# A hybrid decoder trunk whose split weights are made by casting and accumulating transfers

## The chip, the core and the metric

The kernel runs on one core of a Trainium2 chip. The time is device microseconds from launch to end, the median of several runs of the same program; a profile is one further execution under the hardware profiler. Engines are named as in the profile: PE (TensorE), DVE (VectorE), ACT (ScalarE), POOL (GpSimd) and SP (SyncE, which here only issues transfers).

## What is computed

Two layers, each a mixer of four head groups beside each other (retention, differential attention, Mamba-2 SSD, mLSTM) with one input projection and one output projection in common, on 512 tokens of width 1024, all in float32:

```python
for l in range(DEPTH):                      # 2
    u = rmsnorm(h, norm_w[l])
    proj = einsum('bsd,de->bse', u, w_in[l])          # 1024 -> 7696 columns
    ret_p, diff_p, ssd_p, ml_p = split_cols(proj, ...)
    mix = concatenate([ret_out, diff_out, ssd_out, ml_out], axis=-1)   # 2048 columns
    h = h + einsum('bse,ed->bsd', mix, w_out[l])
return rmsnorm(h, final_norm_w)
```

## The kernel before

**Split operands.** The projections' matmuls take operands of the type `float32r`. Each operand is cut in two: a high part, which is the value cast to float32r, and a low part, which is the value less the high part. A product is three matmuls that add up in PSUM: high x high, low x high and high x low. For the activations the parts are `uh` and `ul` (transposed, 8 pieces of 128 features by 512 tokens), or `mh` and `ml` for a mixer's output; for the weights they are `whi` and `wlo`.

**Blocks.** The input projection is cut into 15 blocks of 512 columns; a block is 8 pieces (k = 0 to 7) of 128 x 512. `load_block` (L326) asks `split_w` (L321) for two pieces at a time: one transfer of 512 KB on SP's queue into a tile `raw` (two buffers), then for each piece a cast on ACT into `whi` (L316) and a subtraction into `wlo` (L318), on POOL for even k and on DVE for odd k. `whi` and `wlo` have ten buffers of 128 x 512 each, so ten pieces, 1.25 blocks, can be in the chip. All of it stands at high priority in the scheduler.

**Use.** `proj_tok` (L396) makes a block's output for four tiles of 128 tokens, `proj_feat` (L413) for four tiles of 128 columns. A tile is 24 matmuls of 512 columns into one PSUM bank (`pspj`, two banks), in the order of the pieces: high part with uh, high part with ul, low part with uh, then the next piece. So a piece's buffers are in use from the first tile of a block to its last. An evacuation follows each tile: DVE or ACT reads `pspj`, for instance L478 (a convolution over time), L498 (rotary embedding) or L436 (silu). `out_proj` (L520) works in the same way: for each half of the 1024 output columns 4 pieces, 12 matmuls a tile, and L547 adds the tile to `h`.

**Order.** The program writes out TensorE's order itself: `filler` runs the steps of a layer in the order of the list `ORDER` (mv, gates, mq, mk, mlstm, mo, mz, dk, dq, diff, dv, dz, m, xs, bc, ssd, d, rqk, sz, rv, rz, ret, s, r; the one-letter steps are the output projections), and at each `yield` of a projection the parts of the mixers that have come due are put between its matmuls. The other engines' order is made by a scheduler from priorities; each engine, and each transfer queue, then works through its instructions strictly in that order. In layer 0 the first block (mv, in `start`, L330) is written out by hand on all engines, with its own tiles and a list that says in which order high and low parts are used in the first tile.

Of the kernel before, what the change touches and what calls it, by code (L numbers as in the profile page):

```python
# [11 lines left out]
F32 = mybir.dt.float32  # L12
F32R = mybir.dt.float32r
# [5 lines left out]
P = 128  # L19
# [9 lines left out]
# column offsets of the combined input projection  # L29
# [5 lines left out]
# the 512 column blocks in the order in which they are used  # L35
# [7 lines left out]
# columns of the row parameters that every partition gets  # L43
# [3 lines left out]
# the order of the steps of a layer  # L47
# [3 lines left out]
# the pieces of a block of weights whose low parts GpSimd computes  # L51
POOL_K = (0, 2, 4, 6)

# tiles that hold the queries' parts
QS = 4

# how much work of TensorE is issued before work that depends on other engines
# [5 lines left out]
# columns of the constants  # L63
# [31 lines left out]
class Trunk:  # L95
    def __init__(self, ctx, tc, aps, dbg=None):
        self.tc, self.nc = tc, tc.nc
        self.x, self.win, self.wg, self.wout, self.nrm, self.rows, self.convp, self.cst, self.out = aps
        self.dbg = dbg or {}
        mk = lambda n, b, **k: ctx.enter_context(tc.tile_pool(name=n, bufs=b, **k))  # L100
        self.cp = mk("cp", 1)
        self.pool = mk("pool", 1)
        self.ps = mk("ps", 2, space=bass.MemoryType.PSUM)
        self.n = 0
        # the order of TensorE's work: tasks come due on a clock of emitted TensorE time
        self.clk = 0.0
        self.heap = []
        self.done = set()
# [16 lines left out]
    def spawn(self, gen, delay=0.0):  # L125
        """Runs a generator; what it yields is the delay until it goes on."""
        def step():
            for w in gen:
                self.later(w, step)
                return  # L130
        self.later(delay, step)
# [44 lines left out]
    def setup(self):  # L176
# [13 lines left out]
        # keeps TensorE busy until the first data come in, so that it runs at its full clock  # L190
# [42 lines left out]
    def load_nw(self, l, eng):  # L233
        """The weights of a norm of h, on every partition."""
        self.nw = [self.t("bcm", [P, 512], bufs=2) for _ in range(2)]
        for half in range(2):
            eng.dma_start(out=self.nw[half],
                          in_=self.nrm[l:l + 1, half * 512:(half + 1) * 512].to_broadcast([P, 512]))
# [72 lines left out]
    def split_half(self, raw, j, vector=False):  # L311
        nc = self.nc
        hi = self.t("whi", [P, 512], F32R, bufs=10)
        lo = self.t("wlo", [P, 512], F32R, bufs=10)
# [6 lines left out]
    def split_w(self, src, g):  # L321
        raw = self.t("raw", [P, 2, 512], bufs=2)
        self.nc.sync.dma_start(out=raw, in_=src)
        return [self.split_half(raw[:, j, :], 2 * g + j not in POOL_K) for j in range(2)]

    def load_block(self, name):  # L326
        b = BIDX[name]
        return [q for g in range(4) for q in self.split_w(self.win[self.l, b, :, 2 * g:2 * g + 2, :], g)]

    def start(self, evac):  # L330
        """The first block: the norm of x, and the weights, as they come in."""
# [9 lines left out]
        with self.tc.manual_schedule(engines={E.Activation, E.DVE, E.Pool, E.SP}):  # L341
# [3 lines left out]
            for k in range(KD):  # L345
                if k < 4:
                    if k % 2 == 0:
                        r = self.t("raw", [P, 2, 512], bufs=2)
                        nc.sync.dma_start(out=r, in_=self.win[0, b, :, k:k + 2, :])
                    raw.append(r[:, k % 2, :])  # L350
                else:
                    raw.append(self.t("z", [P, 512], bufs=8))
                    nc.sync.dma_start(out=raw[k], in_=self.win[0, b, :, k, :])
                if k == 3:
                    load(1)
# [4 lines left out]
            # on VectorE or GpSimd  # L360
            split = lambda k, v, h=False: w.append(self.split_half(raw[k], v, h))
            n = [self.norm_in_t(t) for t in range(NT)]
            # the products with the weights' high parts (0) and low parts (1), as these come in
# [32 lines left out]
    def proj_tok(self, name, evac, w=None, toks=range(NT), order=None):  # L396
        nc = self.nc
        w = w or self.load_block(name)
        for t in toks:
# [4 lines left out]
            for k, parts in order or [(k, (0, 1)) for k in range(KD)]:  # L404
                for part in parts:
# [7 lines left out]
    def proj_feat(self, name, evac):  # L413
        nc = self.nc
        w = self.load_block(name)
        for f in range(4):
            p = self.psum("pj")
            fs = slice(f * P, (f + 1) * P)
            for k in range(KD):
                hi, lo = w[k][0][:, fs], w[k][1][:, fs]  # L420
                self.mm(p, lhsT=hi, rhs=self.uh[:, k, :], start=(k == 0), stop=False)
                self.mm(p, lhsT=hi, rhs=self.ul[:, k, :], start=False, stop=False)
                self.mm(p, lhsT=lo, rhs=self.uh[:, k, :], start=False, stop=(k == KD - 1))
                yield
            evac(f, p)

    # evacuations
    def ev_silu(self, dst, tag, bufs, nwt=None):
        """2 * silu(z), times a row weight."""
# [57 lines left out]
    def ev_rope(self, sink, scale=1.0):  # L487
        """Rotates the heads' halves; the features lie on the partitions."""
# [21 lines left out]
    def finish_mix(self, mix):  # L510
        """Transposes of a mixer's output, in high and low parts, for the output projection."""
# [8 lines left out]
    def out_proj(self, g, mixt, tok_outer=False, after=None, cut=False, heads=False):  # L520
        nc = self.nc
        gi = GROUPS[g]
        w = [[x for q in range(2) for x in self.split_w(self.wout[self.l, gi, half, :, 2 * q:2 * q + 2, :], 2 * half + q)]
# [4 lines left out]
        for t, hf in order:  # L528
# [5 lines left out]
            for c0, c1 in zip(cuts, cuts[1:]):  # L534
# [4 lines left out]
                for k in range(4):  # L539
                    hi, lo = w[hf][k]  # L540
                    mh, ml = m(t, k)
                    self.mm(p, lhsT=mh, rhs=hi[:, cs], start=(k == 0), stop=False)
                    self.mm(p, lhsT=ml, rhs=hi[:, cs], start=False, stop=False)
                    self.mm(p, lhsT=mh, rhs=lo[:, cs], start=False, stop=(k == 3))
                    yield
# [15 lines left out]
    def gates(self):  # L561
# [20 lines left out]
        # log1p(exp(-|x|)) = 2 atanh(z / (2 + z)), z = exp(-|x|)  # L582
# [31 lines left out]
        # SSD factors  # L614
# [12 lines left out]
        # rows  # L627
# [19 lines left out]
        # running maxima: rows 0.. G, 32.. mu, 64.. G at the end of the chunk  # L647
# [44 lines left out]
    def bcast(self, src, n, t, tag, bufs):  # L692
        """Rows of src, columns of chunk t, on every partition."""
# [9 lines left out]
    def mlstm(self, v, th, zs, q, k, res):  # L703
# [5 lines left out]
        for t in range(NT):  # L709
# [47 lines left out]
            # denominators  # L757
# [18 lines left out]
            # r / 2 * rsqrt(r^2 / 4 * var + eps)  # L776
# [112 lines left out]
    def retention(self, qk, v, zs, res):  # L889
# [6 lines left out]
        for t in range(NT):  # L896
# [6 lines left out]
            # heads on different rows of the array write different banks  # L903
# [55 lines left out]
    def split_k(self, dst):  # L959
        """High and low parts of a head's keys, one above the other, for each of its two maps."""  # L960
# [13 lines left out]
    def split_q(self, x):  # L974
        """The high parts of a head's queries, on both halves of the partitions, and the low parts."""
# [108 lines left out]
    def layer(self, l, last):  # L1084
        """The steps of a layer that keep TensorE busy, and the mixers that run between them."""
# [40 lines left out]
        def end():  # L1126
# [7 lines left out]
            # mLSTM  # L1134
# [8 lines left out]
            # differential attention  # L1143
# [6 lines left out]
            # SSD  # L1150
# [5 lines left out]
            # retention  # L1156
# [7 lines left out]
    # columns of the last tokens' halves  # L1164
# [34 lines left out]
def _layout(i):  # L1199
    """The inputs, cut and reordered into the pieces that the kernel loads."""  # L1200
# [36 lines left out]
```

## Time and profile before

| | |
|---|---|
| median of 3 runs | 1088.46 us (1086.24 to 1088.56) |
| span of the profiled execution, from its first to its last instruction (the only time known of it) | 1091.0 us |
| mean granted TensorE clock | 0.984 |
| busy: PE, DVE, ACT, POOL | 1043.6, 714.8, 492.0, 392.9 us |
| bytes moved by transfers | 95.53 MB, 88 GB/s over the span |

A group's line in the profile reads: line of the kernel, engine, operation, output<-inputs by the program's names, shapes, count | busy us, mean ns of one | idle us of the engine just before them, and what ended most of it. A line of the timeline reads: start in us, duration, engine, line, operation, count, and in brackets the idle time of that engine before it with its releaser. In the order of instructions, names carry buffer numbers, and an xN at the end stands for N equal instructions in a row.

### The profile page before, as it was taken

The numbers are of one execution on the slowest core, as the hardware profiler recorded it, in microseconds if no ns is written. First come the engines' busy times: TensorE is split into PE (matmuls) and PEld (weight loads), VectorE is DVE, ScalarE is ACT, GpSimd is POOL, SyncE is SP. The second block draws the span as 40 slices with busy tenths as digits, with TensorE's granted clock in tenths as the row PEclk, the third lists the DMA queues.
The fourth block names the chain that finished last, engine by engine and source line by source line (L and its number), as shares of the span: only waits on it lengthen the run. The fifth ranks groups of instructions, "written<-read, shape, count | busy, mean of one in ns | idle before, by whom it ended". The sixth has DMA issues, their size and how long they took to land.

```text
span 1091.0 us, 14197 instructions
## 1 busy us (share of the span) xinstructions
PE 1043.6 (96%) x5052; PEld 848.7 (78%) x5052; DVE 714.8 (66%) x1369; ACT 492.0 (45%) x1082; POOL 392.9 (36%) x369
## 2 busy tenths in 40 slices
PE   7999989999999899999999999999999999999997
PEld 6778878777788787787887788787877877787776
DVE  5686676567787767445556867664687886773454
ACT  4444337655554344332344442484555542543332
POOL 3322445324323354225132234533252343542341
PEclk8999999999999999999999999899999999999999
DMA  7332313321312323332122322222231223223202
GB/s 283 102 100 85 97 49 97 96 77 57 92 46 79 106 68 97 108 119 72 39 82 74 116 89 86 78 77 77 79 101 55 78 87 107 71 85 115 78 20 77
DMA packets 39143, 95.53 MB, mean 88 GB/s; under 512 B 3592, under 2 KB 16520, under 8 KB 38944
## 3 DMA queue, kind: packets, MB, share of 16 engines
q1 hardware_dynamic: 38064, 93.18, 26.8%
q10 hardware_dynamic: 1008, 1.44, 0.4%
q8 instruction: 39, 0.64, 0.2%
q14 instruction: 32, 0.26, 0.1%
HBM read 92.47 MB, written 2.15 MB: 87 GB/s over the span
## 4 chain that ended last, share of the span: by engine, by line
PE 79%; DVE 11%; DMA 3%; issue 3%; ACT 3%; POOL 1%; SPq 0%; ACTq 0%; POOLq 0%; DVEq 0%
PE pspj L115 64%; PE psacc L115 6%; PE psS L115 5%; PE psS L119 4%; DVE wlo L318 3%; DMA raw<-in_w_in_dram 2%; DVE w L826 2%; DVE e L478 1%; ACT whi L316 1%; DMA cst<-in_consts_dram 1%; DVE w L721 0%; ACT e L496 0%; POOL s L207 0%; DVE z L436 0%; DVE ft L498 0%
## 5 line engine op out<-in xcount | busy, mean ns | idle before, releaser
L318 POOL TENSOR_TENSOR wlo<-raw,whi 128x512 fp32r<-128x512 f32 x150 | 206.5, 1380 | 358.8 <-ACT whi L316 231.7
L318 DVE TENSOR_TENSOR wlo<-raw,whi 128x512 fp32r<-128x512 f32 x150 | 173.7, 1159 | 89.4 <-ACT whi L316 76.9
L115 PE MATMUL pspj<-whi,uh 128*128 128x512 f32 x512 | 209.5, 409 | 8.5 <-DVE ft L498 8.2
L316 ACT CAST whi<-raw 128x512 fp32r<-128x512 f32 x300 | 175.8, 619 | 91.9 <-DMA raw<-in_w_in_dram 54.7
L115 PE MATMUL pspj<-whi,ul 128*128 128x512 f32 x512 | 201.8, 394 | 0.0
L115 PE MATMUL pspj<-wlo,uh 128*128 128x512 f32 x512 | 201.5, 395 | 0.2
L115 PE MATMUL pspj<-uh,whi 128*128 128x512 f32 x448 | 182.0, 406 | 9.3 <-DVE e L478 4.9
L115 PE MATMUL pspj<-uh,wlo 128*128 128x512 f32 x448 | 177.3, 396 | 1.2 <-POOL wlo L318 1.2
L115 PE MATMUL pspj<-ul,whi 128*128 128x512 f32 x448 | 176.4, 394 | 0.0
L115 PEld LDWEIGHTS pspj<-whi,uh 128*128 128x128 f32 x512 | 97.6, 191 | 31.0 <-DVE ft L498 9.7
L115 PE MATMUL pspj<-whi,mh 128*128 128x512 f32 (+1 forms) x260 | 107.4, 413 | 10.7 <-DVE h L547 8.0
L115 PEld LDWEIGHTS pspj<-wlo,uh 128*128 128x128 f32 x512 | 96.9, 190 | 22.7 <-DVE wlo L318 1.0
L115 PEld LDWEIGHTS pspj<-whi,ul 128*128 128x128 f32 x512 | 97.8, 191 | 18.2 <-DVE ul L306 0.2
L115 PEld LDWEIGHTS pspj<-uh,whi 128*128 128x128 f32 x448 | 85.6, 191 | 28.9 <-issue 6.1
L115 PE MATMUL pspj<-whi,ml 128*128 128x512 f32 (+1 forms) x260 | 102.2, 393 | 0.0
L115 PE MATMUL pspj<-wlo,mh 128*128 128x512 f32 (+1 forms) x260 | 102.2, 393 | 0.0
L115 PEld LDWEIGHTS pspj<-uh,wlo 128*128 128x128 f32 x448 | 85.4, 191 | 21.1 <-POOL wlo L318 2.5
L115 PEld LDWEIGHTS pspj<-ul,whi 128*128 128x128 f32 x448 | 85.6, 191 | 16.2
L207 POOL TENSOR_TENSOR s<-s,nhalf 128x4 f32<-128x4 f32 (+1 forms) x44 | 36.8, 837 | 160.2 <-DVE s L1058 76.0
L478 DVE SCALAR_TENSOR_TENSOR e<-pspj,cvh,e 128x511 f32<-128x511 f32 (+2 forms) x90 | 66.9, 744 | 14.6 <-ACT e L476 13.5
L115 PEld LDWEIGHTS pspj<-whi,mh 128*128 128x128 f32 x260 | 49.4, 190 | 23.7 <-DVE h L547 10.0
L496 ACT ACTIVATE e<-pspj 32x512 f32<-32x512 f32 x96 | 56.6, 590 | 12.9 <-PE pspj L115 11.4
(213 smaller groups left out, 1490.5 us busy)
## 6 DMA issues: line engine op xcount, KB each, us to landing
raw<-in_w_in_dram SPq DMA_DIRECT2D x118, 512.0 KB, 3.9
raw<-in_w_out_dram SPq DMA_DIRECT2D x32, 512.0 KB, 3.3
bcm<-adr SPq DMA_DIRECT2D x16, 256.0 KB, 3.4
bcm<-gdr SPq DMA_DIRECT2D x8, 256.0 KB, 4.9
out_dram<-z SPq DMA_DIRECT2D x7, 256.0 KB, 2.0
h<-in_x_dram SPq DMA_DIRECT2D x3, 512.0 KB, 8.5
rows<-in_rows_dram SPq DMA_DIRECT2D x2, 592.0 KB, 9.0
cst<-in_consts_dram SPq DMA_DIRECT2D x1, 1035.0 KB, 8.9
```

The source lines that it names most:

```text
L115: self.nc.tensor.matmul(out, lhsT=lhsT, rhs=rhs, start=start, stop=stop, **kw)
L119: self.nc.tensor.transpose(out, src, self.ident if ident is None else ident)
L207: self.nc.gpsimd.tensor_tensor(out=out, in0=m, in1=self.nhalf[:, :n], op=ALU.pow)
L316: (nc.vector.tensor_copy if vector else nc.scalar.copy)(out=hi, in_=raw)
L318: eng.tensor_tensor(out=lo, in0=raw, in1=hi.bitcast(F32), op=ALU.subtract)
L478: nc.vector.scalar_tensor_tensor(acc[:, s:], p[:, 0:S - s], w[:, 3 - s:4 - s], acc[:, s:], ALU.mult, ALU.add)
L496: nc.scalar.activation(x[q * 32:q * 32 + 32, :], p[o * 32:o * 32 + 32, :], AF.Copy, scale=scale)
L826: nc.vector.scalar_tensor_tensor(e[:, j * P:(j + 1) * P], ab[g][:, j, :], self.ncs[:, t, h:h + 1], self.cap, ALU.add, ALU.min)
```

## The change

The parts of the weights, except those of the first block of layer 0, are no longer made by a cast and a subtraction of a tile `raw`:

- The high parts of two pieces come by one transfer on POOL's queue that casts float32 to float32r on the way (`nc.gpsimd.dma_start(out=hi, in_=src)`).
- ACT then writes minus the high part into the low tile, 128 x 1024 at once (`nc.scalar.mul`, L337).
- A second transfer on POOL's queue from the same source adds the weights onto that (`accum_op=ALU.add`, L338), which leaves the value less its high part.
- `raw` goes. `whi` and `wlo` become tiles of two pieces (a pair, 128 x 2 x 512), with 7 and 5 buffers (`WP`).
- In the first tile of a block (of a half, in an output projection) all high parts are used first and the low parts after them; in the last tile the low parts first. The tiles between keep the order by pieces.
- The first block's weights are loaded into tiles of the tags `ft` and `z`, one piece a transfer, and split as before; its order is the same.

```diff
-POOL_K = (0, 2, 4, 6)
+WP = 7, 5
+
+def parts(n, first, last):
+    hi, lo = [[(k, (j,)) for k in range(n)] for j in range(2)]
+    return hi + lo if first else lo + hi if last else [(k, (0, 1)) for k in range(n)]
...
-    def split_half(self, raw, j, vector=False):
-        nc = self.nc
-        hi = self.t("whi", [P, 512], F32R, bufs=10)
-        lo = self.t("wlo", [P, 512], F32R, bufs=10)
+    def pair(self):
+        return [self.t(tag, [P, 2, 512], F32R, bufs=n) for tag, n in zip(("whi", "wlo"), WP)]
+
+    def split_half(self, raw, hi, lo, j, vector=False):
+        nc = self.nc
         with self.tc.high_priority(W["hp"]):
             (nc.vector.tensor_copy if vector else nc.scalar.copy)(out=hi, in_=raw)
...
-    def split_w(self, src, g):
-        raw = self.t("raw", [P, 2, 512], bufs=2)
-        self.nc.sync.dma_start(out=raw, in_=src)
-        return [self.split_half(raw[:, j, :], 2 * g + j not in POOL_K) for j in range(2)]
+    def split_w(self, src):
+        nc = self.nc
+        hi, lo = self.pair()
+        with self.tc.high_priority(W["hp"]):
+            nc.gpsimd.dma_start(out=hi, in_=src)
+            nc.scalar.mul(lo, hi.bitcast(F32), -1.0)
+            nc.gpsimd.dma_start(out=lo, in_=src, accum_op=ALU.add)
+        return [(hi[:, j, :], lo[:, j, :]) for j in range(2)]
...
-            for k, parts in order or [(k, (0, 1)) for k in range(KD)]:
-                for part in parts:
+            for k, ps in order or parts(KD, t == 0, t == NT - 1):
+                for part in ps:
                     for u in (self.uh,) if part else (self.uh, self.ul):
                         n += 1
                         self.mm(p, lhsT=u[:, k, ts_], rhs=w[k][part], start=(n == 1), stop=(n == 3 * KD))
...
-            for k in range(KD):
-                hi, lo = w[k][0][:, fs], w[k][1][:, fs]
-                self.mm(p, lhsT=hi, rhs=self.uh[:, k, :], start=(k == 0), stop=False)
-                self.mm(p, lhsT=hi, rhs=self.ul[:, k, :], start=False, stop=False)
-                self.mm(p, lhsT=lo, rhs=self.uh[:, k, :], start=False, stop=(k == KD - 1))
+            n = 0
+            for k, ps in parts(KD, f == 0, f == 3):
+                for part in ps:
+                    for u in (self.uh,) if part else (self.uh, self.ul):
+                        n += 1
+                        self.mm(p, lhsT=w[k][part][:, fs], rhs=u[:, k, :], start=(n == 1), stop=(n == 3 * KD))
                 yield
...
-                for k in range(4):
-                    hi, lo = w[hf][k]
-                    mh, ml = m(t, k)
-                    self.mm(p, lhsT=mh, rhs=hi[:, cs], start=(k == 0), stop=False)
-                    self.mm(p, lhsT=ml, rhs=hi[:, cs], start=False, stop=False)
-                    self.mm(p, lhsT=mh, rhs=lo[:, cs], start=False, stop=(k == 3))
+                n = 0
+                for k, ps in parts(4, t == 0, t == NT - 1):
+                    for part in ps:
+                        for x in m(t, k)[0:1] if part else m(t, k):
+                            n += 1
+                            self.mm(p, lhsT=x, rhs=w[hf][k][part][:, cs], start=(n == 1), stop=(n == 12))
                     yield
```

More of the change, by code (lines that the diff above doesn't have):

```diff
@@ L319, in split_half @@
         return hi, lo
-    def split_w(self, src, g):
-        raw = self.t("raw", [P, 2, 512], bufs=2)
-        self.nc.sync.dma_start(out=raw, in_=src)
-        return [self.split_half(raw[:, j, :], 2 * g + j not in POOL_K) for j in range(2)]
+    def split_w(self, src):
[6 more added lines that the diff above has]
+        return [(hi[:, j, :], lo[:, j, :]) for j in range(2)]
     def load_block(self, name):
         b = BIDX[name]
-        return [q for g in range(4) for q in self.split_w(self.win[self.l, b, :, 2 * g:2 * g + 2, :], g)]
+        return [q for g in range(4) for q in self.split_w(self.win[self.l, b, :, 2 * g:2 * g + 2, :])]
     def start(self, evac):
@@ L345, in start @@
             for k in range(KD):
[L346 to L353, printed above, removed]
+                raw.append(self.t("ft", [P, 512], bufs=11) if k < 4 else self.t("z", [P, 512], bufs=8))
+                nc.sync.dma_start(out=raw[k], in_=self.win[0, b, :, k, :])
                 if k == 3:
@@ L359, in start @@
             self.loads(0)
-            split = lambda k, v, h=False: w.append(self.split_half(raw[k], v, h))
+            pairs = [self.pair() for _ in range(4)]
+            split = lambda k, v, h=False: w.append(self.split_half(
+                raw[k], *[x[:, k % 2, :] for x in pairs[k // 2]], v, h))
             n = [self.norm_in_t(t) for t in range(NT)]
@@ L522, in out_proj @@
         gi = GROUPS[g]
-        w = [[x for q in range(2) for x in self.split_w(self.wout[self.l, gi, half, :, 2 * q:2 * q + 2, :], 2 * half + q)]
+        w = [[x for q in range(2) for x in self.split_w(self.wout[self.l, gi, half, :, 2 * q:2 * q + 2, :])]
              for half in range(2)]
```

## The prediction

> **What bounds the kernel now.** I read the page's busy shares first, then TensorE's waits, then two stretches of the timeline, then the DMA rows.
>
> ```profile
> span 1091.0 us, 14197 instructions
> ...
> PE 1043.6 (96%) x5052; PEld 848.7 (78%) x5052; DVE 714.8 (66%) x1369; ACT 492.0 (45%) x1082; POOL 392.9 (36%) x369
> ```
>
> TensorE (PE) is busy for 96% of the span. Only 47 us are idle, so no change to the other engines can win more than that, while everything that makes TensorE wait is paid in full. What it waits for now, from the view of waits for that engine (waiting tile, releaser: us in total, times, longest):
>
> ```profile
> PE pspj L115 <- DVE ft L498: 8.7, 6, 2.2
> PE pspj L115 <- DVE h L547: 8.0, 5, 2.5
> PE pspj L115 <- DVE e L478: 4.9, 3, 2.3
> PE pspj L115 <- ACT whi L316: 4.3, 3, 2.0
> PE psS L119 <- DMA cst<-in_consts_dram: 3.0, 1, 3.0
> PE pspj L115 <- DVE z L436: 2.7, 2, 1.3
> ...
> PE pspj L115 <- POOL wlo L318: 1.2, 2, 0.6
> ```
>
> The projections' accumulators (pspj) wait on VectorE (DVE) for 8.7 + 8.0 + 4.9 + 2.7 = 24.3 us: evacuations that come late. The weights themselves hold TensorE for only 4.3 + 1.2 us. One such late evacuation, in order of time (start, duration, engine, line):
>
> ```profile
> 204.62 1.40 DVE L318 TENSOR_TENSOR wlo<-raw,whi 128x512 fp32r<-128x512 f32 x1 [0.35 <-PE pspj L115]
> ...
> 205.94 0.68 DVE L498 SCALAR_TENSOR_TENSOR ft<-pspj,cst 128x512 f32<-128x512 f32 x1
> ...
> 206.67 0.79 PE L115 MATMUL pspj<-whi,uh 128*128 128x512 f32 x1 [2.08 <-DVE ft L498]
> ```
>
> A subtraction for a low part (1.40 us) stands in VectorE's queue ahead of the evacuation, and TensorE idles 2.08 us. What follows such an idle time shows in two windows of 3.4 us, the first begun by that matmul (columns: length, busy time and instructions of each engine, granted clock, DMA share, GB/s):
>
> ```profile
> 206.67:210.08 3.41, 3.41 (x8) 2.73 (x9) 1.36 (x2) 2.15 (x5) 1.63 (x2) 0.52 0.62 214
> 210.50:213.90 3.40, 3.40 (x17) 2.78 (x16) 2.76 (x4) 1.24 (x3) 2.55 (x2) 1.00 0.51 151
> ```
>
> The granted clock is 0.52, and 8 matmuls begin where 17 do otherwise. So a wait of about 2 us costs 3.41 x 0.48 = 1.6 us more. The pace at full clock, from 26 starts in a row:
>
> ```profile
> 93.97 0.39 PE L115 MATMUL pspj<-whi,uh 128*128 128x512 f32 x1
> ...
> 99.86 0.39 PE L115 MATMUL pspj<-wlo,uh 128*128 128x512 f32 x1
> ```
>
> 5.89 us / 26 = 0.2265 us per matmul. A tile of a block (24 matmuls) is 5.4 us, a block 21.7 us.
>
> **What goes and what comes.** The groups that make the parts (busy us, mean ns of one):
>
> ```profile
> L318 POOL TENSOR_TENSOR wlo<-raw,whi 128x512 fp32r<-128x512 f32 x150 | 206.5, 1380 | 358.8 <-ACT whi L316 231.7
> L318 DVE TENSOR_TENSOR wlo<-raw,whi 128x512 fp32r<-128x512 f32 x150 | 173.7, 1159 | 89.4 <-ACT whi L316 76.9
> ...
> L316 ACT CAST whi<-raw 128x512 fp32r<-128x512 f32 x300 | 175.8, 619 | 91.9 <-DMA raw<-in_w_in_dram 54.7
> ```
>
> All but the first block's go: some 169 us from VectorE, 201 us from GpSimd (POOL). ScalarE (ACT) loses some 173 us of casts (296 of the 300) and gets 148 multiplications of 128x1024. Their price from three ACT groups:
>
> ```profile
> L1013 ACT ACTIVATE w<-psS,s 128x512 f32<-128x512 f32 x16 | 10.9, 685 | 4.2 <-DVE s L1012 4.2
> L828 ACT ACTIVATE w<-w 128x512 f32<-128x512 f32 x16 | 10.1, 632 | 22.8 <-DVE w L826 22.7
> ...
> L1013 ACT ACTIVATE w<-psS,s 128x128 f32<-128x128 f32 x16 | 5.7, 364 | 15.8 <-DVE s L1012 15.8
> ```
>
> 685 - 364 = 321 ns for 384 columns, so 632 + 428 = 1.06 us; 148 of them are 157 us, and ScalarE is level. The gain is what TensorE's 24.3 us lose: I take two thirds, **-16 us** (between 0 and -24), since VectorE's part goes but ScalarE's part of each evacuation stays.
>
> The transfers: the queue's packets, MB and share of the 16 engines' span, the groups of issues with median us to landing, and SyncE's issues in one stretch (min/median/max ns):
>
> ```profile
> q1 hardware_dynamic: 38064, 93.18, 26.8%
> ...
> raw<-in_w_in_dram SPq DMA_DIRECT2D x118, 512.0 KB, 3.9
> raw<-in_w_out_dram SPq DMA_DIRECT2D x32, 512.0 KB, 3.3
> ```
> ```profile
> L323 SPq DMA_DIRECT2D raw<-in_w_in_dram x12: 327/328/361, 69.4 to 130.3; - x12
> ```
>
> 26.8% of 1091 us is 292 us for 93.18 MB, so 512 KB keep the 16 engines 1.65 us. The quieter median, 3.3 us to landing, less 0.33 us of issue and 1.65 us of moving, leaves a tail of 1.3 us. Nothing before issues from GpSimd's queue, casts or accumulates in a transfer. I bound these: an issue on GpSimd between SyncE's 0.33 us and GpSimd's own 1.38 us for a 128x512 operation, taken in the middle, 0.85; a casting transfer as a plain one; an accumulating one, which has to fetch the tile as well as the source, between one and two plain ones (1.65 to 3.3 us of the engines), taken in the middle, 2.5. Below the plain price there is no reason to go, since it moves the same bytes and more. On the engines this makes 148 x (1.65 + 2.5) us and some 48 us for the rest, 662 us or 61% of the span: not a bound in itself.
>
> The Trainium skill, "Collectives: The Full Stack", section "The bandwidth ceiling: the fold count and why AG ≠ RS ≠ AR", says that an adding transfer runs at half the rate because the add needs two source reads; by that, an accumulation costs the dear end of my bounds, and the boundary below costs the dear 5.4 us instead of 3.0, which alone adds 24 x 2.4 = 58 us to the sum.
>
> **The path that this opens.** The prefetch has 7 high pairs and 5 low pairs (WP), and a block uses 4. So the next block's high pair 3 takes the place of this block's high pair 0, and its low pairs 1 to 3 those of this block's low pairs 0 to 2. GpSimd's queue where the third block of layer 0 (mk: whi_149 to 155) gives way to the fourth (mo: whi_181 to 187); before:
>
> ```order
> L318 TENSOR_TENSOR wlo_179_717<-raw_177_714,whi_178_716 128x512
> L318 TENSOR_TENSOR wlo_184_727<-raw_182_724,whi_183_726 128x512
> L318 TENSOR_TENSOR wlo_213_891<-raw_211_888,whi_212_890 128x512
> L318 TENSOR_TENSOR wlo_218_901<-raw_216_898,whi_217_900 128x512
> L318 TENSOR_TENSOR wlo_223_911<-raw_221_908,whi_222_910 128x512
> ```
>
> and now:
>
> ```order
> L338 DMA wlo_184_850<-in_w_in_dram 128x1024
> L336 DMA whi_187_859<-in_w_in_dram 128x1024
> L338 DMA wlo_186_855<-in_w_in_dram 128x1024
> L336 DMA whi_271_1123<-in_w_in_dram 128x1024
> L338 DMA wlo_188_860<-in_w_in_dram 128x1024
> ```
>
> The subtractions became transfers, and the last low pair (wlo_188) is issued behind the last high pair and one pair of the block after. TensorE where mo's first tile ends its high parts:
>
> ```order
> L123 MATMUL pspj_189_864<-whi_187_859,uh_1_66 128x512
> L123 MATMUL pspj_189_864<-whi_187_859,ul_2_67 128x512
> L123 MATMUL pspj_189_864<-wlo_182_845,uh_1_66 128x512 x2
> L123 MATMUL pspj_189_864<-wlo_184_850,uh_1_66 128x512 x2
> L123 MATMUL pspj_189_864<-wlo_186_855,uh_1_66 128x512 x2
> L123 MATMUL pspj_189_864<-wlo_188_860,uh_1_66 128x512 x2
> ```
>
> where it had high and low in turn:
>
> ```order
> L115 MATMUL pspj_231_928<-whi_212_890,uh_1_66 128x512
> L115 MATMUL pspj_231_928<-whi_212_890,ul_2_67 128x512
> L115 MATMUL pspj_231_928<-wlo_213_891,uh_1_66 128x512
> L115 MATMUL pspj_231_928<-whi_214_894,uh_1_66 128x512
> L115 MATMUL pspj_231_928<-whi_214_894,ul_2_67 128x512
> ```
>
> The last low pair is now needed 16 + 6 matmuls into the block, 4.98 us after its start T; high pair 3 after 12, at T + 2.72. In the last tile of mk low pair 0 is free after 2 of 24 matmuls, T - 4.98, and high pair 0 after 8 + 4, T - 2.72. From there, with the middle prices:
>
> - low 1: multiplied by T - 3.92, issued by -3.07, on the engines until -0.57.
> - high 3: issued by -1.87, moved until T + 1.08, landed at T + 2.38: in time by 0.3.
> - low 2: moved until 3.58, landed 4.88, where 4.53 is wanted.
> - The next block's high pair: moved until 5.23.
> - low 3: must wait for high 3, so multiplied by 3.44, issued by 4.29, moved until 7.73, landed at T + 9.03: **4.05 us late**.
>
> With the cheap accumulation (1.65) the same steps give 6.48, late by 1.5; with the dear one (3.3) 11.43, late by 6.45. The mixers' matmuls that stand in these windows give some back; each is 0.89 us / 4 = 0.22 us:
>
> ```profile
> 113.85 1.05 PE L115 MATMUL psS<-ft,ft 128*128 128x128 f32 x8
> 114.74 0.60 PE L119 MATMUL psS<-cst,ft 128*128 128x128 f32 x4
> ```
>
> (8 records for 4 matmuls). Counted in TensorE's order, they come to 12.7 us in a layer's twelve windows, 1.06 each. So a boundary costs 3.0 us (0.45 to 5.4). A layer has twelve boundaries of a block behind a block (mv to mq, on to dv to dz, xs to bc, rqk to rv to rz with sz); 24 in all: **+72 us** (11 to 129). At the other 13, around output projections, the high part comes long before, and a low pair takes 1.06 + 0.85 + 2.5 + 1.3 = 5.7 us of the 7.2 or more that the same count gives it: **+3** (0 to 13).
>
> Clock: I let 18 of the 24 waits be long enough, 18 x 1.6 = 29, less some 8 us for late evacuations that bring it about now: **+21** (-8 to +30). The mean granted clock is now
>
> ```profile
> core 0: 1091.0 us, clock 0.984
> ```
>
> which is 1.6% or 17 us lost; 21 us more, of 1171, make it some 0.97.
>
> Queued behind a transfer that waits on GpSimd are the rope products, the mixers' output products and rsqrt; behind a multiplication that waits for high 3 on ScalarE are mk's tanh and mo's first evacuation. They fall into TensorE's own wait, so I add nothing, up to 10 us. The first block is as before, within 1 us.
>
> Sum: 1091.0 - 16 + 72 + 3 + 21 = 1171. The median of the runs, 1088.46, is 2.5 us below the profiled span, the only time that execution has: **1168 us**. Dear end, without the relief: 1091 + 129 + 13 + 30 - 2.5, about 1260. The forecast's own range begins where the waits outweigh the relief, 1091, and ends at 1260.
>
> **The rivals.** *Faster:* all low parts come in time, and only the relief of VectorE is left. It decides from a GpSimd issue of 0.33 us and an accumulation no dearer than a plain transfer: then low 3 lands at T + 5.96, wanted at 4.98 + 1.06 = 6.04. Time: 1091 - 16 - 8 - 2.5 = 1064. For it: the order gives the low parts nearly all the time there is. Against: every price has to be the lowest of its bounds. 0.28. *No change:* gains of 24 eat 24 waits of about 1 us: 1088, 0.05. *The engines are the bound:* from 5.4 us per accumulation on, 148 x (1.65 + 5.4) + 48 fills the span; at four plain transfers, 6.6 us, it is 1270, and 30 us of start make 1300. Against: nothing in the rows costs that. 0.12. The forecast keeps 0.55.
>
> One more rule speaks against the change. VectorE is busy 714.8 us with 1369 operations, 0.52 us each. The Trainium skill, "SBUF — State Buffer", section "SBUF: two separate sides", says that descriptors for GpSimd's transfers can't be written while VectorE, in its two-port modes, holds the port pair that they share; half an operation at two issues per boundary would be 0.5 x 24 = 12 us more, and no row before shows it.
>
> **How the numbers follow.** A measurement can tell about 0.2%, 2.2 us, from no change. Faster 0.28, same 0.05, slower 0.55 + 0.12 = 0.67. The range, 1064 to 1260, reaches from the fast rival to the dear end, and leaves out the bound engines and the quickest part of the fast rival.
>
> **What would show it.** Right: TensorE's waits name transfers into wlo, some 24 of several us in the second half of a block's first tile; a mean clock near 0.97; VectorE near 545 us and the late evacuations fewer; accumulating transfers with more engine time than casting ones. Wrong: waits on low parts below 1 us each (then the fast rival), or DMA shares near 0.9 through whole blocks (the engines), or waits on whi in front of those on wlo (then the casting transfer was mispriced).

## The result, and the profile after

The kernel after takes **1328.28 us** (median of 4 runs, 1324.17 to 1330.27), the kernel before 1087.35 (1086.24 to 1088.56): a ratio of 1.219 [1.215, 1.223]. The direction was forecast, the size was not: 1328 lies outside of the range 1064 to 1260. Times here and below are those of the fast runs: two of experiment 3's four (1203 and 1205 us) and one of experiment 15's four (2064 us) were slow and do not count. The page's span and busy shares, and the clock from the view of cores:

```profile
span 1322.4 us, 13822 instructions
...
PE 1126.2 (85%) x5052; PEld 897.2 (68%) x5052; DVE 529.5 (40%) x1221; ACT 470.7 (36%) x934; POOL 397.8 (30%) x517
```
```profile
core 0: 1322.4 us, clock 0.920
```

TensorE's instructions are the same 5052. Of the 231.4 us that the span grew, its busy time took 82.6 (1043.6 to 1126.2, the same matmuls at a clock of 0.920 instead of 0.984) and its idle time 148.8 (47.4 to 196.2). What it idles for, from the view of waits:

```profile
PE pspj L123 <- DMA wlo<-in_w_in_dram: 101.7, 33, 5.8
PE pspj L123 <- DMA whi<-in_w_in_dram: 46.8, 21, 4.2
PE psacc L123 <- DVE w L921: 8.3, 2, 4.7
PE psS L127 <- ACT w L1025: 7.2, 4, 3.1
PE psS L123 <- DVE ft L495: 5.5, 2, 2.8
PE psacc L123 <- DVE w L740: 4.7, 2, 2.4
PE pspj L123 <- DVE ft L510: 2.2, 4, 0.7
...
PE pspj L123 <- DVE h L559: 0.7, 2, 0.4
```

The two kinds of transfer make 148.5 us in 54 waits, where waits on weights were 5.5 us. By their times they stand at 27 places, all of them in the first tile of a block of the input projection: the 24 boundaries of a block behind a block, with 140.2 us or 5.8 each, and three behind an output projection, with 8.3 together. At all 27 TensorE waits for low pair 3; at 21 of them it has waited for high pair 3 before. The late evacuations have gone from 24.3 to 2.2 + 0.7 us, as forecast, but the mixers' waits in the four rows above theirs (25.7 us) give that back: what TensorE idles for besides weights and late evacuations went from 17.6 to 43.5 us.

One boundary in order of time, from the third block of layer 0 (mk) to the fourth (mo), the one that the prediction worked out. T, the start of mo, is the row at 107.60:

```profile
104.51 0.90 POOL L338 DMA_DIRECT2D wlo<-in_w_in_dram  x1 [13.05 <-ACT wlo L337]
105.40 0.58 POOL L336 DMA_DIRECT2D whi<-in_w_in_dram  x1
106.03 0.87 POOL L338 DMA_DIRECT2D wlo<-in_w_in_dram  x1
...
107.60 0.39 PE L123 MATMUL pspj<-whi,uh 128*128 128x512 f32 x1
...
112.30 1.06 ACT L337 ACTIVATE wlo<-whi 128x1024 fp32r<-128x1024 f32 x1 [3.72 <-DMA whi<-in_w_in_dram]
112.32 0.50 PE L123 MATMUL pspj<-whi,uh 128*128 128x512 f32 x1 [1.84 <-DMA whi<-in_w_in_dram]
...
113.77 0.88 POOL L338 DMA_DIRECT2D wlo<-in_w_in_dram  x1 [6.24 <-ACT wlo L337]
...
114.77 0.73 PE L123 MATMUL pspj<-wlo,uh 128*128 128x512 f32 x2 [0.31 <-DMA wlo<-in_w_in_dram]
119.94 1.22 PE L123 MATMUL pspj<-wlo,uh 128*128 128x512 f32 x2 [4.44 <-DMA wlo<-in_w_in_dram]
```

These are the steps that the prediction wrote down, each later. High pair 3, whose issue began at T - 2.2, landed at T + 4.7 (forecast T + 2.4), 1.84 us after TensorE wanted it. Its negation follows at once, the last accumulation is issued by T + 7.05, and low pair 3 lands at T + 12.3 (forecast T + 9.0). Together TensorE loses 1.84 + 0.31 + 4.44 = 6.6 us here.

Two windows of 3.41 us behind the first and the last of these waits (columns as in the prediction):

```profile
112.32:115.73 3.41, 2.87 (x10) 1.72 (x10) 0.69 (x1) 1.56 (x2) 1.97 (x3) 1.00 1.17 276
119.94:123.35 3.41, 3.41 (x11) 2.92 (x12) 0.00 (x0) 0.60 (x1) 0.00 (x0) 0.50 1.07 275
```

After 1.84 us of waiting the clock was still whole, after 4.44 it was 0.50. The DMA shares of 1.17 and 1.07 say that the 16 engines are full at the boundary, though over the whole span they are at 57%:

```profile
q0 software_dynamic: 42624, 155.21, 52.3%
q1 hardware_dynamic: 17040, 15.58, 3.8%
...
whi<-in_w_in_dram POOLq DMA_DIRECT2D x116, 512.0 KB, 7.9
wlo<-in_w_in_dram POOLq DMA_DIRECT2D x116, 512.0 KB, 7.2
```

GpSimd's queue has 52.3% of 1322.4 us = 692 us of the engines for its 296 transfers. They land 7 to 8 us after their issue begins; the plain ones before took 3.9.

### The profile page after: what moved, and what is told of

Same layout as the page of the kernel before. It is cut to its first block, busy times and chain, and to the rows that moved or that the text cites. A ratio compares the mean times of both kernels' runs of the same rounds, so it can differ in the third digit from the quotient of the medians.

```text
span 1322.4 us, 13822 instructions
## 1 busy us (share of the span) xinstructions
PE 1126.2 (85%) x5052; PEld 897.2 (68%) x5052; DVE 529.5 (40%) x1221; ACT 470.7 (36%) x934; POOL 397.8 (30%) x517
## 3 DMA queue, kind: packets, MB, share of 16 engines
q0 software_dynamic: 42624, 155.21, 52.3%
## 4 chain that ended last, share of the span: by engine, by line
issue 37%; PE 27%; DMA 16%; POOL 14%; DVE 4%; ACT 3%; POOLq 0%; SPq 0%; ACTq 0%; DVEq 0%
PE pspj L123 18%; DMA whi<-in_w_in_dram 7%; DMA wlo<-in_w_in_dram 7%; PE psacc L123 5%; POOL wlo L338 4%; POOL whi L336 3%; PE psS L123 2%; POOL e L511 1%; PE psS L127 1%; POOL s L215 1%; DMA whi<-in_w_out_dram 1%; ACT wlo L337 1%; DVE w L838 1%; ACT e L508 1%; POOL w L865 1%
## 5 line engine op out<-in xcount | busy, mean ns | idle before, releaser
L123 PE MATMUL pspj<-whi,uh 128*128 128x512 f32 x512 | 217.4, 425 | 36.1 <-DMA whi<-in_w_in_dram 32.0
L123 PE MATMUL pspj<-wlo,uh 128*128 128x512 f32 x512 | 186.1, 431 | 62.9 <-DMA wlo<-in_w_in_dram 62.6
L338 POOL DMA_DIRECT2D wlo<-in_w_in_dram x116 | 107.9, 933 | 408.4 <-ACT wlo L337 382.6
L337 ACT ACTIVATE wlo<-whi 128x1024 fp32r<-128x1024 f32 x148 | 152.7, 1055 | 196.0 <-DMA whi<-in_w_in_dram 134.4
L123 PE MATMUL pspj<-whi,ul 128*128 128x512 f32 x512 | 209.0, 408 | 0.2 <-DVE ul L314 0.2
L123 PE MATMUL pspj<-uh,wlo 128*128 128x512 f32 x448 | 158.3, 424 | 39.1 <-DMA wlo<-in_w_in_dram 39.1
L123 PEld LDWEIGHTS pspj<-wlo,uh 128*128 128x128 f32 x512 | 103.8, 207 | 93.8 <-DMA wlo<-in_w_in_dram 71.5
L123 PEld LDWEIGHTS pspj<-uh,whi 128*128 128x128 f32 x448 | 88.9, 199 | 38.3 <-DMA whi<-in_w_in_dram 17.6
L123 PE MATMUL pspj<-wlo,mh 128*128 128x512 f32 (+1 forms) x260 | 87.3, 402 | 0.5 <-DVE h L559 0.4
L336 POOL DMA_DIRECT2D whi<-in_w_in_dram x116 | 82.7, 753 | 10.2 <-PE pspj L123 8.0
L448 DVE SCALAR_TENSOR_TENSOR z<-e,pspj 128x512 f32<-128x512 f32 x32 | 21.9, 686 | 143.1 <-ACT e L446 143.0
```

What stands on the lines that cost most here:

```text
L123: self.nc.tensor.matmul(out, lhsT=lhsT, rhs=rhs, start=start, stop=stop, **kw)
L336: nc.gpsimd.dma_start(out=hi, in_=src)
L337: nc.scalar.mul(lo, hi.bitcast(F32), -1.0)
L338: nc.gpsimd.dma_start(out=lo, in_=src, accum_op=ALU.add)
L448: nc.vector.scalar_tensor_tensor(z, th, 1.0, p, ALU.add, ALU.mult)
```

## The experiments

The first theory was the prediction's chain: at a boundary the high pair lands, then it is negated, then the low pair is accumulated, and each link is longer than assumed. The rivals were the engines' time in the burst, GpSimd's queue, and the order of the pieces itself. Ratios are to the kernel before, with 95% intervals.

**1. The order alone.** The edit in the kernel before, made in all three kinds of projection; one of them:

```diff
-for k, parts in order or [(k, (0, 1)) for k in range(KD)]:
+for k, ps in order or parts(KD, t == 0, t == NT - 1):
```

> Only the order of the pieces is changed in the kernel before: first tile high parts first, last tile low parts first; transfers, casts and subtractions stay. Theory (the transfers' latency along the chain high pair, negation, accumulation makes the wait): the order itself is harmless, 1075 to 1100 us, and weights hold TensorE for under 15 us. Rival (the order itself is at fault, since it frees high parts late and low parts all want to be there at once): over 1150 us, with waits on whi and wlo in every block.

Measured: 1166.48 us, 1.069 [1.066, 1.073]. "Harmless" was wrong, and by some 75 us; the time is the rival's, but TensorE waits on high parts only. Its waits, and one boundary (ScalarE's casts, SyncE's issues, TensorE):

```profile
PE pspj L121 <- ACT whi L322: 58.7, 19, 5.7
```
```profile
93.84 2.18 ACT L322 CAST whi<-raw 128x512 fp32r<-128x512 f32 x4 [1.53 <-PE pspj L121]
96.46 6.88 SPq L329 DMA_DIRECT2D raw<-in_w_in_dram  x3
100.39 1.14 ACT L322 CAST whi<-raw 128x512 fp32r<-128x512 f32 x2 [2.63 <-DMA raw<-in_w_in_dram]
...
101.06 0.50 PE L121 MATMUL pspj<-whi,uh 128*128 128x512 f32 x1 [1.40 <-ACT whi L322]
```

The casts at 93.84 waited for TensorE to give back high buffers, which it now does only in the last two thirds of a block's last tile; the next raw transfers are issued after that, when the subtractions too have given `raw` back, and their casts come when TensorE already waits.

**2. The kernel after in the plain order.**

```diff
-    return hi + lo if first else lo + hi if last else [(k, (0, 1)) for k in range(n)]
+    return [(k, (0, 1)) for k in range(n)]
```

> The kernel after, but every tile takes high and low parts in turn. Theory: a boundary's chain begins some 1.4 us earlier (high pair 0 is free at T - 4.1 instead of T - 2.7) and low pair 3 is wanted 0.5 us earlier, so nearly the same: 1300 to 1350 us. Rival (the order is what hides most of the transfers, and the wait that is left is the rest): 24 boundaries times 3 us more, over 1400 us.

Measured: 1257.74 us, 1.154 [1.148, 1.159], outside of both expectations: the new order costs 70 us here too.

**3. No accumulation.** `accum_op=ALU.add` is dropped from the second transfer, so that the low parts are the whole weights.

> The kernel after with a casting transfer in the place of the accumulating one (the low parts then hold the wrong numbers: the source itself); number, bytes, queue and waits of the transfers stay. Theory of the chain: low pairs 1 and 2 are off the engines sooner, so high pair 3 lands 2 to 3 us sooner, and low pair 3 itself lands 1.5 us sooner, of the 6.2 us per boundary some 3.5 go: 1328 - 24 x 3.5 = 1244, some less with the clock, 1210 to 1260 us. Rival (the engines' time of the burst alone sets the wait: with about half of it gone, nothing is left): 1080 to 1150 us. Rival (the issue on GpSimd and the waits of its queue, not the transfers): over 1300 us.

Measured: 1189.84 us, 1.091 [1.084, 1.097]: 138 us less than after, more than the chain's 70 to 120, and far from nothing left. The waits on high pairs fell from 46.8 to 14.3 us, those on low pairs from 101.7 to 56.7.

**4. No chain.**

```diff
-nc.scalar.mul(lo, hi.bitcast(F32), -1.0)
+nc.scalar.mul(lo, self.c(C_DEC, 1024).rearrange("p (j c) -> p j c", j=2), -1.0)
```

> The kernel after, but the negation reads a constant tile instead of the high part, so that a low pair need not wait for its high pair (the low parts then hold wrong numbers); every transfer, its size and its accumulation stay. Theory of the chain: low pair 3 is issued near T - 2 and lands near T + 5.5 where T + 5 is wanted, nearly all of the 24 x 6.2 us goes, and with it most of the half clock: 1130 to 1180 us. Rival (the engines' time of the burst: three accumulations and a cast at 3.4 and 1.8 us are 12 us from T - 3 on): low pair 3 still lands near T + 9, a third goes at most, 1260 to 1310 us.

Measured: 1187.23 us, 1.090 [1.085, 1.094], 141 us less than after, near the chain's side but not at it. High pairs are still waited for:

```profile
PE pspj L123 <- DMA whi<-in_w_in_dram: 37.5, 19, 4.2
PE pspj L123 <- DMA wlo<-in_w_in_dram: 30.0, 25, 2.2
```

So the chain explains most of the waits on low pairs. Those on high pairs shrink without the accumulation (14.3 us in experiment 3), and in the plain order of experiment 2 there are none.

**5. Neither chain nor accumulation** (both edits).

> The kernel after with neither chain nor accumulation: the negation reads a constant tile and the second transfer casts (the low parts hold wrong numbers), order and buffers stay. New theory (the order shortens the time of a high pair from 8.2 us, buffer free at T - 4.1 and wanted at T + 4.1, to 5.4 us, T - 2.7 to T + 2.7; chain and accumulation come on top of that): low pairs are in time, high pair 3, with a landing of 5 to 6 us behind its issue, is late by 1 to 2 us, 1100 to 1140 us. Rival (chain and accumulation are all of it): 1065 to 1085 us, the kernel before without late evacuations.

Measured: 1100.60 us, 1.010 [1.006, 1.015], as the new theory had it (waits on high pairs 13.8 us, on low pairs 3.3). Seen from here, the chain without the accumulation costs 89 us (experiment 3), the accumulation without the chain 87 (experiment 4), and both 228 of the 241 us that were lost: each makes the other's part larger.

**6. The same in the plain order** (the edit of 2 on top).

> As the run before, and every tile takes high and low parts in turn as in the kernel before. New theory of the order: 8.2 us for each pair cover issue and landing, 1065 to 1085 us. Rival (transfers issued by GpSimd, with its issue of about 0.75 us each and its own work in the same queue, cost by themselves): over 1110 us in spite of the plain order.

Measured: 1114.65 us, 1.022 [1.017, 1.027]. My 1065 to 1085 failed, and the time is the rival's: TensorE waits 40.3 us on low pairs and not at all on high ones. So the order that costs 70 us with chain and accumulation is worth 14 us without them. It gives a low pair more time and a high pair less; by the steps of the prediction the chain takes the low pair's gain away, because that pair cannot start before its high pair has landed.

**7 and 8. Two more high buffers for the order.** In the kernel of experiment 1, `bufs=10` becomes 12 for `whi` and 8 for `wlo`; in 8 also `POOL_K = (0, 1, 2, 4, 5, 6)`.

> The kernel before with the new order, and two buffers of 512 columns moved from the low parts to the high ones (12 and 8 instead of 10 and 10). New theory (the order costs because the high pair's buffer comes free late, and with it the cast, the raw buffer and the next transfer): with three pairs' casts ahead or free to go, waits on whi all but vanish, 1085 to 1105 us against the 1166 of the order with 10 and 10. Rival (the order costs because the eight low parts of a block are made and wanted in one burst): 1150 us or more, with waits on wlo.

> The run before, and GpSimd makes six of a block's eight low parts instead of four. A candidate for beating both kernels: VectorE loses half of its 150 subtractions and with them half of the late evacuations' 24 us; 1070 to 1095 us if GpSimd's six subtractions of 1.4 us fit the 9 us from a low part's free buffer to its use; over 1110 us, with waits on wlo, if they don't.

Measured: 1177.47 us, 1.080 [1.077, 1.083], and 1213.06 us, 1.113 [1.110, 1.117]. Both expectations failed; the times are those of the rivals, but the waits on wlo that these named are not there. Waits in experiment 7 (the first by ScalarE, the others by TensorE):

```profile
ACT whi L322 <- DMA raw<-in_w_in_dram: 184.8, 91, 7.3
...
PE pspj L121 <- ACT whi L322: 19.8, 20, 2.0
PE pspj L121 <- DVE h L554: 16.4, 6, 3.9
PE pspj L121 <- DVE ft L505: 11.0, 12, 1.6
```

The waits on high parts did go, 58.7 to 19.8 us, and late evacuations came instead. ScalarE now waits 184.8 us with a cast at the head of its queue (73.8 in experiment 1); that the evacuations are held up behind such casts fits, but was not tried by itself.

**9. Eight high pairs and four low ones** in the kernel after: `WP = 8, 4`.

> The kernel after with 8 high and 4 low pairs instead of 7 and 5, all else as it is: a whole block's high pairs are ahead, so that no low pair waits for a transfer at the boundary. Theory (the new order holds high buffers to the end, and the chain hands that lateness on to the low parts): waits on whi vanish, and the wait on the last low pair shrinks as it did when the chain was cut: 1160 to 1240 us. Rival (four accumulations, now all at the boundary, are 11 us of the engines from T - 4 on, and that sets the end whatever the chain): 1280 to 1340 us.

Measured: 1298.62 us, 1.190 [1.184, 1.195]: the rival's time. No wait on a high pair is left, yet

```profile
PE pspj L123 <- DMA wlo<-in_w_in_dram: 104.1, 59, 3.1
PE pspj L123 <- DMA wlo<-in_w_out_dram: 20.8, 8, 3.4
```

With no high pair late, but with all four accumulations in the burst, the loss is nearly the same. A late high pair is thus not needed for it. Since this kernel also has one low pair fewer ahead, the run does not tell the accumulations' price from that of the missing buffer, and a low pair here still has its negation between its free buffer and its transfer.

**10. The queue alone.** In the kernel before:

```diff
-self.nc.sync.dma_start(out=raw, in_=src)
+with self.tc.high_priority(W["hp"]):
+    self.nc.gpsimd.dma_start(out=raw, in_=src)
```

> The kernel before, its plain transfers issued by GpSimd instead of SyncE; nothing else. If a transfer by GpSimd's queue lands later by itself (issue near 0.75 us, landing 5 to 6 us instead of 3.9): 1100 to 1150 us, as the plain order with two casting transfers showed. Rival (the later landings are those of casts and accumulations that crowd the engines): landing stays near 4 us and the time within 1% of before, 1080 to 1100 us.

Measured: 1132.35 us, 1.037 [1.034, 1.041], with the time of the first expectation and the landing of the second:

```profile
span 1127.8 us, 14166 instructions
...
q0 software_dynamic: 21312, 77.60, 21.8%
...
raw<-in_w_in_dram POOLq DMA_DIRECT2D x116, 512.0 KB, 4.2
```

21.8% of 1127.8 us for 148 transfers is 1.66 us each, as before, and 4.2 us to landing against 3.9. A plain transfer is not slower by GpSimd's queue; the 40 us come from elsewhere, most likely from standing in line with GpSimd's own work.

**11. Casting alone**, in the order of before, with `WP = 5, 5` and two raw pairs:

```diff
+raw = self.t("raw", [P, 2, 512], bufs=2)
+nc.sync.dma_start(out=raw, in_=src)
 nc.gpsimd.dma_start(out=hi, in_=src)
-nc.scalar.mul(lo, hi.bitcast(F32), -1.0)
-nc.gpsimd.dma_start(out=lo, in_=src, accum_op=ALU.add)
+for j in range(2):
+    (nc.vector if j else nc.gpsimd).tensor_tensor(out=lo[:, j, :], in0=raw[:, j, :],
+                                                  in1=hi[:, j, :].bitcast(F32), op=ALU.subtract)
```

> One part of the change alone, in the order of before and with its buffers (5 pairs each and two raw pairs): high parts by casting transfers, low parts still by subtraction, from a raw pair that SyncE fetches as before. A casting transfer of about 6 us from T - 4.1 + 0.75 on and a subtraction of 1.4 us end near T + 4.0, wanted from T + 4.1 on: 1085 to 1120 us. If casting transfers are the costly part of the change: over 1160 us, with waits on wlo behind whi.

Measured: 1242.72 us, 1.139 [1.132, 1.146]; 1085 to 1120 failed. The time is the rival's, but not for its reason:

```profile
q0 software_dynamic: 21312, 77.60, 20.7%
...
raw<-in_w_in_dram SPq DMA_DIRECT2D x116, 512.0 KB, 4.0
whi<-in_w_in_dram POOLq DMA_DIRECT2D x116, 512.0 KB, 4.7
```
```profile
PE pspj L123 <- POOL wlo L340: 64.0, 37, 4.9
...
POOL whi L338 <- PE pspj L123: 164.0, 67, 15.6
POOL wlo L340 <- DMA whi<-in_w_in_dram: 94.2, 64, 5.9
```

The casting transfer is cheap: 20.7% of 1239.3 us / 148 = 1.73 us of the engines, landed in 4.7. What is late is GpSimd: it stands 164 us with a transfer at the head of its queue that waits for TensorE to give a buffer back, and 94.2 us with a subtraction that waits for a casting transfer to land; TensorE waits 64 us for subtractions from that same queue. How the 150 us divide between the two was not tried.

**12. Accumulating alone**, with the same buffers and order:

```diff
-nc.gpsimd.dma_start(out=hi, in_=src)
+raw = self.t("raw", [P, 2, 512], bufs=2)
+nc.sync.dma_start(out=raw, in_=src)
+nc.scalar.copy(out=hi, in_=raw)
 nc.scalar.mul(lo, hi.bitcast(F32), -1.0)
 nc.gpsimd.dma_start(out=lo, in_=src, accum_op=ALU.add)
```

> The other part alone, in the order of before and with its buffers: high parts cast by ScalarE from a raw pair that SyncE fetches, low parts by negation and accumulating transfer. High pair 3 is cast by T - 0.3 (its buffer is free at T - 1.4), negated by T + 0.8, issued by T + 1.7, landed 6 to 7 us later, T + 8, wanted at T + 4.5: 3.5 us late, with the half clock behind it some 5 us in each of 24 boundaries, less 16 us for VectorE: 1160 to 1230 us. Rival (only both kinds of transfer together crowd the engines): under 1120 us.

Measured: 1381.73 us, 1.266 [1.261, 1.270], above both expectations, and slower than the whole change (which has seven high pairs for the five here).

```profile
span 1381.3 us, 13953 instructions
...
q0 software_dynamic: 21312, 77.60, 30.3%
...
raw<-in_w_in_dram SPq DMA_DIRECT2D x116, 512.0 KB, 7.1
wlo<-in_w_in_dram POOLq DMA_DIRECT2D x116, 512.0 KB, 9.3
```

30.3% of 1381.3 us / 148 is 2.83 us of the engines for an accumulation, 1.7 times a plain transfer. (That is the sum of all its packets; the median 4096-byte packet of the trace took 328 ns, 2.1 times the 159 ns of a plain one.) And the plain transfers beside them, on SyncE's queue and unchanged, land after 7.1 us; beside the casting ones they took 4.0. Both runs move the same bytes, so the accumulations are dear in themselves and slow what moves with them.

**13 and 14. Half of the order each**, in the kernel after: `return hi + lo if first else ...` in 13, `return lo + hi if last else ...` in 14, other tiles plain.

> The kernel after with only the first tile's half of the order (low parts last); the last tile takes them in turn. If the last tile's half is at fault (it gives high pair 0 back 1.4 us later, and with the chain the last low pair as well, while the first tile's half gives each low pair up to 3.6 us more): 1225 to 1270 us, like the kernel after in the plain order (1258) or below. If the first tile's half is at fault (all high pairs wanted by T + 2.7): 1300 to 1350 us.

> The kernel after with only the last tile's half of the order (low parts first); the first tile takes them in turn. If the last tile's half is at fault: 1300 to 1360 us. If the first tile's half is: 1225 to 1270 us.

Measured: 1273.79 us, 1.169 [1.164, 1.174], and 1341.77 us, 1.232 [1.225, 1.239]. 13 lies just above its range, 14 in the one for a fault of the last tile's half. Against 1258 for the plain order the first tile's half costs 16 us and the last tile's 84. The waits of 14 are on low pairs (165.9 us, on high pairs 1.6). By the prediction's steps, what hurts is that the last tile keeps high pair 0 until T - 2.7 instead of T - 4.1, with the chain behind it. With both halves it is 70 us: beside the last tile's half the first tile's gives some back.

**15. Output projections only.** In the kernel before, with its order and its buffers, only the 32 pairs of the output projections come by the two new transfers.

> The kernel before (its order, its five pairs of buffers each, its SyncE transfers, casts and subtractions for the input projections); only the 32 pairs of the output projections come by casting and accumulating transfers. If these are in time there, as in the kernel after (no wait of note on them): VectorE loses 32 of 150 subtractions, 1080 to 1095 us, at best a little under before. If the accumulations hold up the plain transfers beside them, as where they came alone: 1100 to 1150 us.

Measured: 1164.83 us, 1.068 [1.065, 1.072], above both expectations. Waits, landings:

```profile
PE pspj L124 <- DMA wlo<-in_w_out_dram: 42.3, 8, 6.3
```
```profile
whi<-in_w_out_dram POOLq DMA_DIRECT2D x32, 512.0 KB, 4.8
wlo<-in_w_out_dram POOLq DMA_DIRECT2D x32, 512.0 KB, 5.6
```

With few of them about, a casting pair lands in 4.8 us and an accumulating one in 5.6; with only five pairs of buffers and the plain order that is still late: 8 waits of 5.3 us, as many as there are output projections. No kernel of this study was faster than the kernel before, and none of the runs points to one that would be.

## Why the prediction was wrong

**Right.** It named the bound (TensorE) rightly, the place (boundaries from a block to a block), the last link (low pair 3 behind the negation of high pair 3, waited for at all 27 places), and the output projections: their own tiles never wait for weights, and the three places behind them cost 8.3 us (+3 forecast, 0 to 13). The prices on the processors held: the negation took 1.055 us (1.06 forecast), an issue of an accumulation 0.93 us (0.85), VectorE fell to 529.5 us (545). On the engines a casting transfer does cost nearly what a plain one does, 1.73 against 1.65 us. The rows of the issue and of the negation:

```profile
L338 POOL DMA_DIRECT2D wlo<-in_w_in_dram x116 | 107.9, 933 | 408.4 <-ACT wlo L337 382.6 <-ACT g L694 14.2 <-ACT s L281 5.7
...
L337 ACT ACTIVATE wlo<-whi 128x1024 fp32r<-128x1024 f32 x148 | 152.7, 1055 | 196.0 <-DMA whi<-in_w_in_dram 134.4
```

**The failed step: "So a boundary costs 3.0 us", 24 of them +72.** The 24 boundaries cost 140.2 us, 5.8 each. Three things in that term were mis-sized.

- *The time from issue to landing.* I took 0.85 + 2.5 + 1.3 = 4.65 us for an accumulation and 0.85 + 1.65 + 1.3 = 3.8 for a cast. Where little else moves (experiment 15) they take 5.6 and 4.8. The tail is therefore not the 1.3 us of the plain transfers of before: 5.6 - 0.9 - 2.83 leaves 1.9. The engines' part was short too, 2.5 for 2.83; with 2.83 and 1.73 the same steps give a boundary of 4.1 us instead of 3.0 (an estimate).
- *The crowd.* I let transfers follow one another at their own prices. At the boundary the engines are full (DMA shares of 1.17 and 1.07), and landings become 7 to 9 us, those of plain transfers too (experiment 12).
- *High pair 3, "landed at T + 2.38: in time by 0.3".* That step is where both enter first: it lands 2.3 us later than worked out, 21 high pairs make TensorE wait (46.8 us), and the whole lateness is handed down the chain. The prediction named waits on whi as a sign that the casting transfer was mispriced. On the engines it was not: 1.73 us. What stands in front of it there is an accumulation, and without the accumulations the waits on whi fall to 14.3 us and the kernel by 138 us (experiment 3).

**The clock: +21 forecast, 82.6 us more busy time measured.** The trace's clock records hold TensorE at half clock for 213 us of the span, 177 of them busy; in the kernel before, for 37 and 29. Half of the 148 us more is 74 of the 82.6. I took 1.6 us for 18 waits, one to a boundary. Half clock went with the long waits: at all 25 waits on weights of more than 3 us the clock was at half when TensorE went on or within 1.4 us of it, at the 29 shorter ones only 7 times. And it stayed there for more than the 3.41 us of the price: in the boundary above from 117.69 to 124.52, 4.58 us of that after the wait had ended. The price itself rested on one row; of the kernel before's own waits, those that end at 419.23 (1.98 us) and 603.47 (2.27 us) left the clock at 1.00 for the next 3.41 us.

**The relief: -16 forecast.** The rows that I meant lost 21.4 us, and 25.9 us of other waits, most of them the mixers', came in their place. The prediction had no term for what is late next among the mixers. Nor were the 47 idle us the most that other engines could win, as it said: the 17 us lost to the clock stand beside them.

**What was not asked.** The order was taken as part of the scenery. It is a cost of its own: 75 us in the kernel before, 70 in the kernel after (there its last-tile half alone costs 84), although it is worth 14 us once chain and accumulation are gone. It was not needed for the number, since the steps were written down with it, but I expected it to be harmless, and only the run showed otherwise.

**The rivals.** "Faster" would have needed an accumulation at the plain price; it is 1.7 times that, and even with a cast in its place and no chain the kernel takes 1100.6 us (experiment 5). "The engines are the bound" is wrong over the whole span (57%) and right inside the boundary's windows; experiment 9 shows that side, where four accumulations in the burst, with one low pair fewer ahead, cost nearly the same without any late high pair.

**The two rules.** The Trainium skill, "Collectives: The Full Stack", section "The bandwidth ceiling: the fold count and why AG ≠ RS ≠ AR", has the adding transfers of a reduce-scatter at half the rate of copies. The median packet agrees (328 ns against 159); the engines' time, 1.7 times, lies between that and my 1.5, and nearer to mine. The dear boundary of 5.4 us that I worked out from it is near the 5.8 measured, but the reason differs: the price alone makes 4.1 (the estimate above), and the rest is later landing. The Trainium skill, "SBUF — State Buffer", section "SBUF: two separate sides", has descriptors for GpSimd's transfers held up while VectorE is in its two-port modes. Here the issue of a casting transfer took 0.75 us in the kernel after, with VectorE busy for 530 us, and 0.58 in experiment 11, with VectorE busy for 704: no sign of it in the length of an issue.

What stays open: how the loss divides between the chain and the engines' burst, since each grows with the other (89 and 87 alone, 228 together), and why the order with two more high buffers did not recover (7 and 8).

## What to carry to other kernels

Where the work of a boundary moves from processors to transfers, price each transfer from issue to landing in the crowd that it will meet, not in the quiet of before, and count every long wait it makes: here each of the 25 of more than 3 us had its stretch at half clock. Transfers that depend on each other (a load, then an accumulation onto it) need buffers that come free early for the first of them; an order that holds exactly those buffers to the end undoes what it gives to the second. A transfer put into a processor's in-order queue waits there for its buffer in front of that processor's own work (164 us in experiment 11).

## What was not expected of the hardware

- An accumulating transfer of 512 KB takes 2.83 us of the 16 engines (experiment 12), a casting one 1.73 (11), a plain one by GpSimd's queue 1.66 (10).
- Plain transfers of another queue land at 7.1 us while accumulations run (12), at 4.0 while casting transfers do (11).
- A plain transfer issued by GpSimd lands 4.2 us after its issue begins, against 3.9 by SyncE: the queue itself costs little.
- In the kernel without the chain, GpSimd stood before transfers for which the profile names nothing that they wait for, 43 times, up to 3.3 us; what holds them was not tried:

```profile
POOL whi L336 <- issue: 65.6, 43, 3.3
```
